# A mixture-of-experts tail: where the one-hot selection, the scatter-adds and the loads of the sums stand in the queues

## The chip, the cores and the metric

One Trainium2 chip, one of its cores. The metric is the device time of one execution in microseconds (us), of which the median of several runs is given. Engines are called TensorE (PE in the profile), VectorE (DVE), ScalarE (ACT), GpSimd (POOL) and SyncE (SP). TensorE has a second row, PEld, for its weight loads. Each engine takes its instructions in order from a queue of its own; SyncE's and POOL's queues also issue the DMA transfers.

## The reference

One block of a streaming encoder over 512 tokens of width 1024 in float32: a mixer of two branches (chunked retention and sparse attention), then a hierarchical mixture of experts, then a last RMSNorm. The change concerns the experts and the last norm:

```python
# u2: normalized tokens; 16 experts in 4 groups; top group, then its top 2 experts
gates = einsum('tke,tk->te', one_hot(eid, 16), wts)      # zero for 14 of 16 experts
a = einsum('td,edf->tef', xb, w1)                         # 1024 -> 256
b = einsum('td,edf->tef', xb, w3)
hid = silu(a) * b * gb[:, :, None]
y   = einsum('tef,efd->td', hid, w2)                      # 256 -> 1024
h = h + g2 * y
out = rmsnorm(h, norm_final_g)
```

Each token goes to two experts, so an expert has 64 tokens on the average. The weights of one expert are 3 MB (w1, w3 and w2 of 1 MB each).

## The kernel before

**Planner.** The kernel records its instructions in a list and does not emit them as they are written. A planner (`Program.run`) gives each one an engine time and a DMA time from a table of costs (`cost`), plays the whole list through in its own model of the engines and the DMA, and so fixes for every engine the order of its queue and for every tile the place in on-chip memory. Lower `prio` (recorded earlier) goes first among instructions that could start at about the same time. A tile has a "tag" with places for it; places of different phases may overlap, and a later phase opens when the tiles of the earlier one are done. What the planner assumes of time decides only the order; on the chip each queue waits for what is really ready.

**Router.** For each of four blocks of 128 tokens the kernel computes the block's sum `hh` (stored to `hrow` in DRAM, 512 rows of 1024) and the normalized tokens (stored to `u2row` as a high and a low half in float16), and picks experts. At its end, `row_all` holds for each expert the list of its token numbers (128 slots, unused ones out of bounds) and `gate_all` the gates.

**Experts.** The loop at L1334 runs over 16 experts. `load` fetches an expert's weights from SyncE's queue as three tiles of 1 MB (two with half of w1 and w3 each, one with w2) and splits each on ScalarE and VectorE into two float16 parts. `compute` gathers the expert's tokens from `u2row` by an indirect DMA from POOL's queue into one of six buffers `xg`, transposes them, runs gate and up matmuls, SiLU and product, two transposes, the down matmuls, and scales the result into a tile `y`. `add` is an indirect DMA from POOL that adds the rows of `y` to the rows of `hrow` that `row` names (a scatter-add). `hrow` is split into four views so that experts which follow each other use different views; two scatter-adds to one view wait for each other.

In the kernel before, only the scatter-adds of experts 0 and 1 (in loop order) are issued as they come. Those of 2 to 14 are kept in a list `late` and recorded behind an instruction `gated` on POOL that reads the last expert's w2 tile, so that they start when the last weights have arrived:

```python
1338        if i == E - 1 and late:
1339            R.hold = gated = POOL.tensor_copy(gate[0:1, 0:1], raw[0:1, 0:1])
1340            for a in late:
1341                add(*a)
...
1344        if 2 <= i < E - 1:
1345            late.append((y, row, hrow_of[e // 4]))
```

The tiles `y` that wait for them have nine places (three, two, and four over the buffers `xg`).

**The last expert** has no scatter-add. Its `y` stays on chip and is added by a matmul with a one-hot selection: `last` holds the numbers 0 to 511 along the row (`iota` on POOL, a copy to float on VectorE), and `at_last` is 1 where that number equals the token number in a slot of the last expert (`is_equal` on VectorE). These instructions are recorded after the loop (L1353 to L1359).

**Branch.** At L1367 every engine reads the number of rounds; L1368 branches over a block that serves experts with more than 128 tokens. With this input the block is skipped. Instructions behind it are planned on their own.

**Final norm** (L1388 to L1407), for each block of 128 tokens: SyncE loads the sums from `hrow`, TensorE multiplies the selection by `y` (float32), VectorE adds the product to the sums, ScalarE squares and sums, POOL takes the power -0.5, and VectorE, ScalarE and POOL scale the block, which SyncE stores.

Of the kernel before, what the change touches and what calls it, by code (L numbers as in the profile page):

```python
# [11 lines left out]
F32 = mybir.dt.float32  # L12
F16 = mybir.dt.float16
I32 = mybir.dt.int32
AF = mybir.ActivationFunctionType
OP = mybir.AluOpType
# [4 lines left out]
S = 512  # L21
D = 1024
KT = D // 128
NT = S // 128
H = 8
E = 16
# [122 lines left out]
class Program:  # L149
# [149 lines left out]
    def cost(self, op, method, a, k, reads, writes):  # L299
        ap = lambda v: v.ap if isinstance(v, View) else v  # L300
        ps = lambda v: isinstance(v, View) and v.buf.tag.space == "PS"
        op.dma = 0.0
        out = ap(writes[0])
        n = shape_of(out)
        if "dma" in method:
            tot = cnt = 0
            for v in (writes[0], [r for r in reads][0]):
                x = ap(v)
                e = mybir.dt.size(x.dtype)
                tot_v = 1  # L310
                for c in x.shape:
                    tot_v *= c
                tot = tot_v if not tot else min(tot, tot_v)
                run = x.shape[-1] if list(x.ap)[-1][0] == 1 else 1
                cnt = max(cnt, tot_v / run)
            tot *= mybir.dt.size(out.dtype)
            op.dma = max(tot, cnt * 157) / 360.0
            op.dur = 1040.0 if "indirect" in method else 550.0
            return
        if op.eng == "PE":  # L320
            op.share = 1.0
            f32 = ap(reads[0]).dtype == F32
            if method == "transpose":
                op.dur = 109.0 if f32 else 56.0
            else:
                op.dur = max(27.0, n / 2.4 * (4 if f32 else 1) + 2.5)
                if f32 and (n < 128 or out.shape[0] == 64):
                    op.dur = 117.0
                op.share = min(1.0, n / 2.4 * (4 if f32 else 1) / op.dur)
            return  # L330
        big = max([n] + [shape_of(ap(r)) for r in reads if r is not None])
        scal = sum(1 for r in reads[1:] if shape_of(ap(r)) == 1 and n > 1)
        if op.eng == "ACT":
            op.dur = (52.0 if ps(reads[0]) else 93.0) + big / 1.2 + 93 * scal + (93 if "accum_out" in k else 0)
            func = a[2] if len(a) > 2 else k["func"]
            op.table = TABLE.get(func)
        elif op.eng == "DVE":
            two = sum(1 for r in reads if shape_of(ap(r)) > 1) > 1
            half = all(ap(r).dtype == F16 for r in reads)
            fast = not two and (half or not any(ps(v) for v in reads)) and method in ("tensor_scalar", "tensor_copy", "memset")  # L340
            op.dur = 69.0 + big * (0.52 if fast else 1.042) + 61 * min(1, scal)
        else:
            if k.get("op") == OP.pow:
                op.dur = 300 + 165.0 * n
            elif method in ("memset", "iota", "tensor_scalar"):
                op.dur = 60 + 0.87 * n
            else:
                op.dur = 150 + 2.1 * n
# [150 lines left out]
KB = 1024  # L499
ARENA = 207 * KB  # L500
NXG = 6


def block(ctx, tc, A, out):
# [3 lines left out]
    dram = ctx.enter_context(tc.tile_pool(name="scratch", bufs=1, space=DRAM))  # L508
# [3 lines left out]
    R = Program(tc, arena, banks)  # L512
    R.TABLE_COST = 300
    T = R.tile
# [3 lines left out]
    def stt(o, a, s, b, op0, op1, **k):  # L518
        return DVE.scalar_tensor_tensor(o, a, s, b, op0=op0, op1=op1, **k)
# [12 lines left out]
    hrow = dram.tile([S, D], F32, name="hrow")  # L532

    hrow_of = dram_disjoint_views(hrow, 4)

    x_t = A["x"].rearrange("b (t p) d -> (b t) p d", p=128)
    w_in = A["w_in"].rearrange("l (k p) n -> p (l k) n", p=128)
# [10 lines left out]
    def fixed(shape, dt=F32, phase=0, n=1):  # L548
        size = (2 if dt == F16 else 4) * int(np.prod(shape))
        size += -size % 32  # L550
        t = R.tag("SB", size, (place[phase], n, phase))
        place[phase] += n * size
        return T(t, shape, dt) if n == 1 else t
# [40 lines left out]
    tHH = R.tag("SB", 4 * KB, (U, 2, 4))  # L594
    tG1 = R.tag("SB", 4 * KB, (TMP + 32 * KB, 1, 3))
    tVEC = R.tag("SB", 4 * KB, (U + 16 * KB, 3, 4))
    tT4 = R.tag("SB", 4 * KB, (U + 28 * KB, 3, 4), (U + 40 * KB, 2, 5), (U, 4, 6))
    tWX = R.tag("SB", 8 * KB, (TMP + 64 * KB, 1, 3), (U + 40 * KB, 1, 3), (U + 8 * KB, 1, 4))
    tT4H = R.tag("SB", 4 * KB, (TMP + 40 * KB, 4, 4))
    tSA = R.tag("SB", 2 * KB, (TMP + 36 * KB, 2, 4))  # L600
# [690 lines left out]
    def load(es, early=0):  # L1291
        R.shift, R.low = early, True
        c13 = [split(echunk(w1[:, es, q * 4:q * 4 + 4], w3[:, es, q * 4:q * 4 + 4]), view=paired) for q in range(2)]
        raw = echunk(w2[:, es])
        c2 = split(raw)
        R.shift, R.low = 0, False
        return c13, c2, raw
# [30 lines left out]
    def add(y, row, rows):  # L1328
        POOL.indirect_dma_start(out=rows[:, :], out_offset=Off(row), in_=y, in_offset=None,
                                bounds_check=S - 1, oob_is_err=False, compute_op=OP.add)  # L1330


    late, gate = [], fixed([1])
    for i in range(E):  # L1334
        e = i % 4 * 4 + i // 4
        row = row_all[:, e:e + 1]
        *w, raw = load(slice(e, e + 1), 300 if i < 5 else -50)
        if i == E - 1 and late:
            R.hold = gated = POOL.tensor_copy(gate[0:1, 0:1], raw[0:1, 0:1])
            for a in late:  # L1340
                add(*a)
            R.hold = None
        y = compute(*w, row, gate_all[:, e:e + 1], xg[i % NXG], T(tG1, [D]) if i == E - 1 else None)
        if 2 <= i < E - 1:
            late.append((y, row, hrow_of[e // 4]))
        elif i < E - 1:
            add(y, row, hrow_of[e // 4])

    R.hold = gated
    gfb = T(tVEC, [D])  # L1350
    row_load(gfb, A["norm_final_g"][None, :])
    R.hold = None
    last = T(tVEC, [2, S])  # L1353
    POOL.iota(last[:, 0].bitcast(I32), pattern=[[1, S]], base=0, channel_multiplier=0)
    DVE.tensor_copy(last[:, 1], last[:, 0].bitcast(I32))
    rowf = fixed([1])
    DVE.tensor_copy(rowf, row)
    at_last = last[:, 0]
    DVE.tensor_scalar(at_last, last[:, 1], rowf, None, op0=OP.is_equal)  # L1359
    R.keep(gfb)  # L1360
    R.keep(last)
    assert place[0] <= 8 * KB and place[4] <= ARENA, place
    R.run()

# [1 line left out]
    R.immediate = True  # L1366
    nr = nc.values_load(R.real(nri[0:1, 0:1]), min_val=1, max_val=ROUNDS)  # L1367
    with tc.If(nr > 1):  # L1368
        with tc.For_i(1, nr):
            DVE.tensor_scalar(rank, rank, -128.0, None, op0=OP.add)  # L1370
            pr, pg = psf(), psf()
            for t in range(NT):
                locate(pr, t, val, F16, t == 0, t == NT - 1)
                locate(pg, t, gval, F32, t == 0, t == NT - 1)
            take(pr, pg)
            SP.dma_start(more_row.rearrange("n p -> p n"), row_all)
            SP.dma_start(more_gate.rearrange("n p -> p n"), gate_all)
            with tc.For_i(0, E) as e:
                row, gt = row_all[:, 0:1], gate_all[:, 0:1]
                SP.dma_start(row, more_row.rearrange("n p -> p n")[:, bass.ds(e, 1)])  # L1380
                SP.dma_start(gt, more_gate.rearrange("n p -> p n")[:, bass.ds(e, 1)])
                add(compute(*load(bass.ds(e, 1))[:2], row, gt, xg[0]), row, hrow)
    R.immediate = False


    R.patience = 100
    o_t = out.rearrange("b (t p) d -> (b t) p d", p=128)
    for t in range(NT):  # L1388
        h3 = T(tW8, [2, D], F32, "h")
        SP.dma_start(h3[:, 0], hrow[t * 128:(t + 1) * 128, :])  # L1390
        for n in range(2):
            d = slice(n * 512, (n + 1) * 512)
            p = (psm, psm, psa, psf)[t]()
            PE.matmul(p, at_last[:, t * 128:(t + 1) * 128], y[:, d], start=True, stop=True)
            DVE.tensor_add(h3[:, 0, d], h3[:, 0, d], p)
            ACT.activation(h3[:, 1, d], h3[:, 0, d], AF.Square, accum_out=s3[:, t, n:n + 1])
        DVE.tensor_scalar(s3[:, t, 0:1], s3[:, t, 0:1], 1.0 / D, 1e-6, op0=OP.mult, op1=OP.add)
        stt(s3[:, t, 1:2], s3[:, t, 1:2], 1.0 / D, s3[:, t, 0:1], OP.mult, OP.add)
        POOL.tensor_tensor(s3[:, t, 1:2], s3[:, t, 1:2], mhalf, op=OP.pow)
        for n in range(2):  # L1400
            d = slice(n * 512, (n + 1) * 512)
            if n and t < NT - 1:
                ACT.activation(h3[:, 1, d], h3[:, 0, d], AF.Copy, scale=s3[:, t, 1:2])
                POOL.tensor_mul(h3[:, 1, d], h3[:, 1, d], gfb[:, d])
            else:
                stt(h3[:, 1, d], h3[:, 0, d], s3[:, t, 1:2], gfb[:, d], OP.mult, OP.mult)
            SP.dma_start(o_t[t][:, d], h3[:, 1, d])  # L1407
    R.run()


# [20 lines left out]
```

## Time and profile before

| | before |
|---|---|
| median of 3 runs | 722.64 us (719.57, 722.64, 724.06) |
| profiled execution | 719.95 us |
| span of its profile, first to last instruction | 718.1 us |
| busy: TensorE, VectorE, ScalarE, POOL | 638.4, 552.3, 375.7, 100.3 us |
| mean granted TensorE clock | 0.956 |
| DMA moved | 151.93 MB, 212 GB/s over the span |

How to read the lines that follow: the page has one line for each group of equal instructions and a table in which the span is cut into 40 equal slices (a digit is the busy share in tenths). A line of the timeline has start, duration, engine, source line, operation, output and input with their shapes, count, and in brackets how long the engine had stood idle before and what released it. All tiles on chip are named arena, all accumulators banks; nearly every instruction carries line L494, where the planner emits it. A line of the table of windows has, for a stretch of time, the busy time and count of each engine, then the granted clock, the mean busy share of the 16 DMA engines and the GB/s.

### The profile page before, as it was taken

How to read it: one execution, taken by the hardware profiler on the slowest of the kernel's cores; microseconds unless marked ns; L12 is line 12 of the kernel's file. 1: busy time of each engine (PE TensorE's matmuls, PEld its weight loads, DVE VectorE, ACT ScalarE, POOL GpSimd, SP SyncE). 2: the span in 40 equal slices, each digit the busy share in tenths (PEclk: the TensorE clock that was granted, in tenths of full speed). 3: DMA queues.
4: the chain of work that ended last, by engine and by line, in shares of the span. 5: the costliest groups of instructions: out<-in, count | busy, mean ns of one | idle time of the engine just before them, and what ended most of it. 6: DMA issues, size and time to landing. Idle time of an engine off the chain costs nothing. (4 is left out here: it accounts for less than half of the span.)

```text
span 718.1 us, 10181 instructions
## 1 busy us (share of the span) xinstructions
PE 638.4 (89%) x3673; PEld 345.5 (48%) x3673; DVE 552.3 (77%) x1056; ACT 375.7 (52%) x605; POOL 100.3 (14%) x87
## 2 busy tenths in 40 slices
PE   3799998989999999999799999989559989999942
PEld 2345465747565644555354444435244445555410
DVE  3997699999994677989588545778764788899726
ACT  5457623333253356773475432544347578899304
POOL 1001010111011100000000000041642201102733
PEclk9799999999999999999999999999859999999987
DMA  9998525272265278657758435824628899997546
GB/s 298 359 341 240 170 68 153 64 221 84 73 208 157 78 252 257 222 177 269 217 197 302 177 118 178 327 82 159 222 84 306 273 354 357 375 346 279 101 87 233
DMA packets 85255, 151.93 MB, mean 212 GB/s; under 512 B 10433, under 2 KB 50834, under 8 KB 85074
## 3 DMA queue, kind: packets, MB, share of 16 engines
q1 hardware_dynamic: 80690, 143.21, 59.6%
q0 software_dynamic: 4464, 8.04, 4.7%
q8 instruction: 29, 0.48, 0.3%
q14 instruction: 24, 0.20, 0.1%
q10 hardware_dynamic: 48, 0.00, 0.0%
HBM read 137.91 MB, written 16.81 MB: 215 GB/s over the span
## 5 line engine op out<-in xcount | busy, mean ns | idle before, releaser
L494 PE MATMUL banks<-arena 128*128 128x512 f16 (+9 forms) x3673 | 638.4, 335 | 66.4 <-DVE arena L494 43.3
L494 PEld LDWEIGHTS <-arena 128*128 128x128 f16 x3078 | 282.1, 100 | 289.1 <-issue 32.9
L494 ACT ACTIVATE arena<-arena 128x1024 f16<-128x1024 f32 (+8 forms) x320 | 258.1, 846 | 192.1 <-DVE arena L494 94.0
L494 DVE SCALAR_TENSOR_TENSOR arena<-arena 128x1024 f16<-128x1024 f32 (+7 forms) x318 | 294.0, 949 | 62.9 <-ACT arena L494 48.4
L494 ACT ACTIVATE arena<-banks 128x512 f32<-128x512 f32 (+7 forms) x178 | 99.3, 604 | 106.7 <-PE banks L494 105.5
L494 DVE SCALAR_TENSOR_TENSOR arena<-banks,arena 128x512 f32<-128x512 f32 (+9 forms) x147 | 89.2, 629 | 44.6 <-PE banks L494 30.7
L494 PEld LDWEIGHTS banks<-arena 128*128 128x128 f32 (+2 forms) x595 | 69.3, 168 | 69.4 <-DVE arena L494 38.0
L494 POOL TENSOR_TENSOR arena<-arena 128x512 f32<-128x512 f32 (+2 forms) x36 | 41.7, 1160 | 291.5 <-DVE arena L494 237.3
L494 DVE TENSOR_TENSOR arena<-arena 128x512 f32<-128x512 f32 (+6 forms) x100 | 56.0, 571 | 9.2 <-POOL arena L494 5.8
L494 ACT ACTIVATE arena<-banks,arena 128x128 f32<-128x128 f32 (+1 forms) x48 | 22.9, 531 | 37.1 <-DVE arena L494 25.1
L494 DVE TENSOR_SCALAR arena<-arena 128x1 f32<-128x1 f32 (+7 forms) x76 | 22.6, 328 | 11.8 <-ACT arena L494 5.7
L494 POOL DMA_INDIRECT hrow<-arena x15 | 26.3, 1753 | 19.6 <-DVE arena L494 15.3
L494 DVE MAX8 arena<-arena 128x8 f32<-128x256 f32 (+3 forms) x52 | 27.6, 530 | 1.4
L494 POOL DMA_INDIRECT arena<-u2row,arena x16 | 19.3, 1208 | 62.6 <-PE banks L494 50.1
L494 POOL IOTA arena<- 128x4 int32 (+2 forms) x3 | 1.5, 502 | 188.8 <-PE banks L494 188.7
L494 DVE MATCH_REPLACE8 arena<-arena 128x256 f32<-128x256 f32 (+3 forms) x56 | 27.2, 487 | 0.0
L494 DVE SCALAR_TENSOR_TENSOR arena<-arena,banks 128x512 f32<-128x512 f32 x17 | 11.6, 685 | 7.0 <-PE banks L494 4.5
L494 DVE CUSTOM_DVE_ANT_0 arena<-arena 128x128 f32<-128x128 f32 (+3 forms) x32 | 14.3, 483 | 0.0
L494 POOL MEMSET arena<- 128x2048 f16 (+2 forms) x12 | 11.0, 955 | 7.3 <-PE banks L494 5.0
L494 ACT ACTIVATION_READ_ACCUMULATOR arena<-arena 128x1 f32 x56 | 10.5, 188 | 0.0
L494 DVE TENSOR_TENSOR arena<-arena,banks 128x512 f32<-128x512 f32 (+1 forms) x12 | 6.0, 512 | 5.6 <-DMA arena<-hrow 5.5
L494 DVE BATCH_NORM_STATS2 arena<-banks 128x6 f32<-128x128 f32 x32 | 7.1, 285 | 3.3 <-PE banks L494 3.2
(19 smaller groups left out, 37.4 us busy)
## 6 DMA issues: line engine op xcount, KB each, us to landing
arena<-in_w_ada SPq DMA_DIRECT2D x16, 1024.0 KB
arena<-in_w_exp_gate SPq DMA_DIRECT2D x32, 512.0 KB
arena<-in_w_exp_up SPq DMA_DIRECT2D x32, 512.0 KB
arena<-in_w_exp_down SPq DMA_DIRECT2D x16, 1024.0 KB
arena<-in_w_in SPq DMA_DIRECT2D x14, 1024.0 KB
arena<-in_w_ada SPq DMA_DIRECT2D x4, 2048.0 KB
arena<-in_w_gate SPq DMA_DIRECT2D x8, 1024.0 KB
arena<-arena SPq DMA_DIRECT2D x112, 64.0 KB
```

Of the source, the lines that this page charges most:

```text
L494: o.call(*[self.real(x) for x in o.args], **{n: self.real(x) for n, x in o.kw.items()})
```

## The change

It does six things.

1. The one-hot selection of the last expert (`iota`, copy, `is_equal`) is recorded ahead of the loop over the experts, from the last column of `row_all`.
2. `late` stays empty: each of the 15 scatter-adds is recorded right behind its expert.
3. The loads of the sums from `hrow` become four tiles `ha`, recorded behind the loop and ahead of the branch, in a place of 16 KB that the gather buffers `xg` 2 to 5 leave free; so experts 14 and 15 gather into `xg` 0 and 1, and the tiles `y` lose the four places there.
4. The final norm works on `ha` and keeps only its output in a tile of its own.
5. In the skipped block, later rounds add into a second DRAM table `mrow`, which is then added to `ha`.
6. The planner counts half the DMA time for an indirect transfer.

```diff
@@ cost
-            op.dma = max(tot, cnt * 157) / 360.0
+            op.dma = max(tot, cnt * 157) / 360.0 * (0.5 if "indirect" in method else 1.0)
@@ tags
-    tT4 = R.tag("SB", 4 * KB, (U + 28 * KB, 3, 4), (U + 40 * KB, 2, 5), (U, 4, 6))
+    tT4 = R.tag("SB", 4 * KB, (U + 28 * KB, 3, 4), (U + 40 * KB, 2, 5))
+    tHA = R.tag("SB", 4 * KB, (U, 4, 6))
@@ ahead of the loop
+    last = T(tVEC, [2, S])
+    POOL.iota(last[:, 0].bitcast(I32), pattern=[[1, S]], base=0, channel_multiplier=0)
+    DVE.tensor_copy(last[:, 1], last[:, 0].bitcast(I32))
+    rowf = fixed([1])
+    DVE.tensor_copy(rowf, row_all[:, E - 1:E])
+    at_last = last[:, 0]
+    DVE.tensor_scalar(at_last, last[:, 1], rowf, None, op0=OP.is_equal)
@@ loop over the experts
-        if i == E - 1 and late:
+        if i == E - 1:
             R.hold = gated = POOL.tensor_copy(gate[0:1, 0:1], raw[0:1, 0:1])
...
-        y = compute(*w, row, gate_all[:, e:e + 1], xg[i % NXG], T(tG1, [D]) if i == E - 1 else None)
-        if 2 <= i < E - 1:
+        y = compute(*w, row, gate_all[:, e:e + 1], xg[i % NXG if i < 14 else i - 14], T(tG1, [D]) if i == E - 1 else None)
+        if 15 <= i < E - 1:
             late.append((y, row, hrow_of[e // 4]))
...
-    last = T(tVEC, [2, S])
-    POOL.iota(last[:, 0].bitcast(I32), pattern=[[1, S]], base=0, channel_multiplier=0)
...
-    DVE.tensor_scalar(at_last, last[:, 1], rowf, None, op0=OP.is_equal)
+    ha = [T(tHA, [D]) for _ in range(NT)]
+    for t in range(NT):
+        SP.dma_start(ha[t], hrow[t * 128:(t + 1) * 128, :])
@@ final norm
-        h3 = T(tW8, [2, D], F32, "h")
-        SP.dma_start(h3[:, 0], hrow[t * 128:(t + 1) * 128, :])
+        h3, o3 = ha[t], T(tW8, [D], F32, "h")
...
-            DVE.tensor_add(h3[:, 0, d], h3[:, 0, d], p)
+            DVE.tensor_add(h3[:, d], h3[:, d], p)
```

More of the change, by code (lines that the diff above doesn't have):

```diff
@@ L534, in block @@
     hrow_of = dram_disjoint_views(hrow, 4)
+    mrow = dram.tile([S, D], F32, name="mrow")
     x_t = A["x"].rearrange("b (t p) d -> (b t) p d", p=128)
@@ L1352, in block @@
     R.hold = None
-    last = T(tVEC, [2, S])
-    POOL.iota(last[:, 0].bitcast(I32), pattern=[[1, S]], base=0, channel_multiplier=0)
[L1355 to L1358, printed above, removed]
-    DVE.tensor_scalar(at_last, last[:, 1], rowf, None, op0=OP.is_equal)
-    R.keep(gfb)
-    R.keep(last)
+    ha = [T(tHA, [D]) for _ in range(NT)]
+    for t in range(NT):
+        SP.dma_start(ha[t], hrow[t * 128:(t + 1) * 128, :])
+    for v in (gfb, last, *ha):
+        R.keep(v)
     assert place[0] <= 8 * KB and place[4] <= ARENA, place
@@ L1368, in block @@
     with tc.If(nr > 1):
+        zero = T(tW8, [D])
+        DVE.memset(zero, 0.0)
+        for t in range(NT):
+            SP.dma_start(mrow[t * 128:(t + 1) * 128, :], zero)
         with tc.For_i(1, nr):
@@ L1381, in block @@
                 SP.dma_start(gt, more_gate.rearrange("n p -> p n")[:, bass.ds(e, 1)])
-                add(compute(*load(bass.ds(e, 1))[:2], row, gt, xg[0]), row, hrow)
+                add(compute(*load(bass.ds(e, 1))[:2], row, gt, xg[0]), row, mrow)
+        for t in range(NT):
+            m = T(tW8, [D])
+            SP.dma_start(m, mrow[t * 128:(t + 1) * 128, :])
+            DVE.tensor_add(ha[t], ha[t], m)
     R.immediate = False
@@ L1394, in block @@
             PE.matmul(p, at_last[:, t * 128:(t + 1) * 128], y[:, d], start=True, stop=True)
-            DVE.tensor_add(h3[:, 0, d], h3[:, 0, d], p)
-            ACT.activation(h3[:, 1, d], h3[:, 0, d], AF.Square, accum_out=s3[:, t, n:n + 1])
+            DVE.tensor_add(h3[:, d], h3[:, d], p)
+            ACT.activation(o3[:, d], h3[:, d], AF.Square, accum_out=s3[:, t, n:n + 1])
         DVE.tensor_scalar(s3[:, t, 0:1], s3[:, t, 0:1], 1.0 / D, 1e-6, op0=OP.mult, op1=OP.add)
@@ L1402, in block @@
             if n and t < NT - 1:
-                ACT.activation(h3[:, 1, d], h3[:, 0, d], AF.Copy, scale=s3[:, t, 1:2])
-                POOL.tensor_mul(h3[:, 1, d], h3[:, 1, d], gfb[:, d])
-            else:
-                stt(h3[:, 1, d], h3[:, 0, d], s3[:, t, 1:2], gfb[:, d], OP.mult, OP.mult)
-            SP.dma_start(o_t[t][:, d], h3[:, 1, d])
+                ACT.activation(o3[:, d], h3[:, d], AF.Copy, scale=s3[:, t, 1:2])
+                POOL.tensor_mul(o3[:, d], o3[:, d], gfb[:, d])
+            else:
+                stt(o3[:, d], h3[:, d], s3[:, t, 1:2], gfb[:, d], OP.mult, OP.mult)
+            SP.dma_start(o_t[t][:, d], o3[:, d])
     R.run()
```

## The prediction, made before the changed kernel ran

> **What bounds the kernel now.** I read the page's head and its table of 40 slices first. A slice is 18 us; the digits are busy tenths.
>
> ```profile
> span 718.1 us, 10181 instructions
> ...
> PE   3799998989999999999799999989559989999942
> ...
> DMA  9998525272265278657758435824628899997546
> ...
> GB/s 298 359 341 240 170 68 153 64 221 84 73 208 157 78 252 257 222 177 269 217 197 302 177 118 178 327 82 159 222 84 306 273 354 357 375 346 279 101 87 233
> ```
>
> From slice 32 to slice 35 (574 to 646 us, in the expert stage) TensorE is at 8 or 9 and the DMA engines are at 9. Then the DMA row falls to 7, 5, 4, and TensorE's to 4 and 2 in the last two slices: there is an end in which nobody works much. A table of windows says how much:
>
> ```profile
> 541.00:660.00 119.00, 114.73 (x679) 59.18 (x678) 95.85 (x110) 94.56 (x116) 15.08 (x12) 0.99 0.93 341
> 660.00:684.00 24.00, 23.50 (x131) 11.38 (x129) 17.43 (x22) 11.58 (x16) 18.42 (x11) 1.00 0.49 87
> 684.00:691.00 7.00, 0.00 (x0) 0.00 (x0) 1.58 (x4) 0.05 (x1) 3.91 (x4) 0.83 0.58 103
> ```
>
> Until 660 the DMA engines are 93% busy with expert weights (341 GB/s). From 660 to 684 TensorE works off a backlog (23.50 of 24 us) while the DMA moves 87 GB/s. From 684 to 691 TensorE does nothing at all. The timeline of that end names who holds what:
>
> ```profile
> 659.74 0.98 POOL L494 COPY arena<-arena 1x1 f32<-1x1 f32 x1 [43.79 <-ACT arena L494]
> ...
> 660.90 2.43 POOL L494 DMA_INDIRECT hrow<-arena  x1 [0.17 <-DVE arena L494]
> ...
> 673.05 1.22 DVE L494 SCALAR_TENSOR_TENSOR arena<-arena 128x1024 f16<-128x1024 f32 x1
> ...
> 678.92 0.75 DVE L494 SCALAR_TENSOR_TENSOR arena<-banks,arena 128x512 f32<-128x512 f32 x1 [1.26 <-PE banks L494]
> ...
> 683.67 0.38 ACT L494 ACTIVATE arena<-banks 128x256 f32<-128x256 f32 x1 [6.46 <-PE banks L494]
> 687.24 1.55 POOL L494 DMA_INDIRECT hrow<-arena  x1 [0.93 <-DMA hrow<-arena]
> 688.24 1.15 POOL L494 IOTA arena<- 128x512 int32 x1
> 689.42 0.43 DVE L494 CAST arena<-arena 128x512 f32<-128x512 int32 x1 [9.75 <-POOL arena L494]
> 689.76 0.74 DVE L494 SCALAR_TENSOR_TENSOR arena<-banks,arena 128x512 f32<-128x512 f32 x1
> ...
> 690.79 1.57 POOL L494 DMA_INDIRECT hrow<-arena  x1 [1.40 <-DVE arena L494]
> 690.82 0.41 DVE L494 SCALAR_TENSOR_TENSOR arena<-banks,arena 128x256 f32<-128x256 f32 x1
> ...
> 696.71 0.75 DVE L494 SCALAR_TENSOR_TENSOR arena<-banks,arena 128x512 f32<-128x512 f32 x1 [0.33 <-PE banks L494]
> 697.65 7.13 PE L494 MATMUL banks<-arena 128*128 128x512 f32 x16 [0.98 <-DVEq L1368]
> 699.15 1.77 SPq L494 DMA_DIRECT2D arena<-hrow  x4
> ...
> 703.01 1.28 DVE L494 TENSOR_TENSOR arena<-arena,banks 128x512 f32<-128x512 f32 x2 [5.54 <-DMA arena<-hrow]
> ...
> 711.62 3.08 DVE L494 SCALAR_TENSOR_TENSOR arena<-arena 128x512 f32<-128x512 f32 x3 [0.33 <-POOL arena L494]
> ```
>
> Thirteen scatter-adds start at 660.90, once the last expert's down weights have arrived (the COPY at 659.74 waits for them), and leave one after the other; the twelfth is issued at 687.24. Behind it in POOL's queue stands the iota for the one-hot selection. VectorE reached the copy of that iota after 679.67 and stood 9.75 us. Behind the copy in VectorE's queue waited (a) the second half of expert 14's output, issued at 689.76, without which the last scatter-add could not leave at 690.79, and (b) the last expert's SiLU product, ready when ScalarE was done at 684.05 and run only at 690.82. Then two things join in the first addition at 703.01: the sums by token, loaded at 699.15 after the last scatter-add had landed, and the selection matmuls from 697.65. The load is the later one (VectorE idle 5.54 us, released by DMA arena<-hrow). From 703.01 to the end of the span is 15.1 us of final norm and stores. So the end is bound by a queue: scatter-adds, iota, copy, expert 14, scatter-add, load.
>
> **The change part by part.**
>
> *The selection moves to the router's end.* Three operations leave the end: iota (1.15 us), its copy (0.43) and the comparison (0.47). At the router's end POOL and VectorE have these gaps:
>
> ```profile
> 529.51 1.83 POOL L494 DMA_INDIRECT arena<-u2row,arena  x1 [10.31 <-DVE arena L494]
> 539.91 2.36 DVE L494 SCALAR_TENSOR_TENSOR arena<-arena 128x1024 f16<-128x1024 f32 x2 [5.06 <-ACT arena L494]
> ```
>
> POOL was idle 10.31 us ahead of the first gather, VectorE 5.06 us ahead of 539.91. Lower bound of the cost 0, upper 2.05 us if all three stood one behind the other on the router's chain; I take 0, because those gaps are longer. If they were placed inside the router's dependent chain instead, the 2.05 us would be paid once. What goes: (a) expert 14's second half runs about 1.3 us after its first, at 680.3, not 689.76; (b) the last SiLU product runs at 684.1, not 690.82, and everything that follows from it (transposes, down projection, 697.46) comes 6.7 us earlier: output complete at 690.75, selection matmuls from 690.95, the first sum possible at 691.9 (two of the sixteen, 7.13 us for all).
>
> *Every scatter-add is issued at once.* The number of scatter-adds stays 15; thirteen lose the wait for the last weights and run behind their expert's output, on POOL between the gathers. The last one then leaves at about 680.5, and lands as before:
>
> ```profile
> L494 POOL DMA_INDIRECT hrow<-arena x15: 1552/1569/2426, 554.4 to 690.8; - x15
> ...
> DMA to landing us min/median/max: 5.9/9.2/9.8
> ```
>
> It took 8.3 us from 690.79 to the loads' issue at 699.15 (the rows above: 5.9 to 9.8, median 9.2). So the loads could go at about 688.9, less if fewer scatter-adds are in flight.
>
> *The loads of the sums stand ahead of the branch.* The same four; the first one's data came 3.86 us after issue (699.15 to 703.01), so at 692.7. SyncE then passes the branch behind them; behind it a consumer waits on the producer's own event at the branch, as the selection matmuls do above (released by DVEq L1368):
>
> ```profile
> L1368 SPq EVENT_SEMAPHORE  x8: 17/17/17, 657.1 to 661.2; - x8
> L1368 DVEq EVENT_SEMAPHORE  x1: 21/21/21, 697.6 to 697.6; - x1
> ```
>
> SyncE's eight collect the loads in flight, from 657.1 to 661.2; VectorE's is one of 21 ns. Bounds for the first addition: 0 if it waits only for its own load, 3.0 us more if for all four (the rest of 2 MB at the roughly 400 GB/s below takes about that). I take 0.8, nearer to the first, as the eight are passed one by one in order.
>
> *What the scatter-adds do to the weight stream.* This is the cost. They used to run when DMA was half idle; now eleven of them (experts 2 to 12) fall into the stream ahead of the last gate and up load. What one costs in engine time:
>
> ```profile
> 556.00:560.00 4.00, 4.00 (x20) 1.86 (x19) 3.48 (x5) 2.46 (x4) 1.11 (x2) 1.00 0.38 74
> 560.00:564.00 4.00, 4.00 (x40) 2.68 (x38) 3.64 (x5) 2.84 (x5) 2.15 (x2) 1.00 0.91 271
> 564.00:568.00 4.00, 4.00 (x21) 1.79 (x19) 3.34 (x5) 3.52 (x4) 0.94 (x1) 1.00 0.95 228
> 568.00:572.00 4.00, 4.00 (x24) 2.00 (x23) 3.12 (x3) 1.06 (x1) 0.00 (x0) 1.00 1.01 403
> 584.00:588.00 4.00, 4.00 (x21) 1.92 (x20) 3.95 (x5) 2.16 (x3) 0.00 (x0) 1.00 0.97 329
> ```
>
> The first scatter-add ran nearly alone from 556 to 560: 0.38 of 4 us, so 1.5 us. The second was in flight beside weights from 560 to 568: 7.44 us of busy time (0.91 and 0.95 of 4 us) for 2.0 MB, where the rate of the next row (403 at 1.01, so 399 GB/s) needs 5.0. Lost 2.4 us, plus 0.66 for its own quarter of a MB: 3.1 at most. The row 584 to 588 loses 0.6 without a scatter-add, in a burst of new loads, so 2.5 is fairer; a gather was in flight as well. I take 2.2, nearest to that loaded row. Eleven of them: 24 us of engine time; of the 8.3 us that the engines idled between 541 and 660 I let 3 be filled. The last gate and up load came about 657.1 (1 MB of down weights, 2.6 us at 399 GB/s, ahead of 659.74) and comes about 678. Behind it lie two halves to split (1.05 us on ScalarE, 1.22 on VectorE each, some 3.5 in a pipe) and six matmuls: TensorE could end the last expert's gate and up at 683.5, and its own backlog ends at 683.64. **The cover is the 24 us backlog of TensorE, and it is just used up.** The down weights land one load later and are needed only at 685.7. On top, one stall of this kind has been seen:
>
> ```profile
> 573.53 2.00 ACT L494 ACTIVATE arena<-arena 128x1024 f16<-128x1024 f32 x2 [3.29 <-DMA arena<-in_w_exp_gate]
> 576.32 24.03 PE L494 MATMUL banks<-arena 128*128 128x128 f32 x132 [3.18 <-DVE arena L494]
> ```
>
> ScalarE stood 3.29 us at the head of its queue for a weight load, a SiLU waited behind it, and TensorE lost 3.18 us. With later loads this comes back; bounds 0 and several times 3.2. I take 2 us in all.
>
> The Trainium skill, page "DMA: Bandwidth & Descriptors", section "Issuing engines are not separate DMA queues", says that DMAs from whatever engine end on the same 16 engines and interleave. It speaks against the change, and the trace agrees (228 GB/s at a 0.95 share beside a scatter-add, 403 without). Were it otherwise, the stream would not move and the sum below would be that of the first rival.
>
> *The planner's figure* (half the transfer time for indirect DMAs), the places of buffers and the second table for later rounds add no instruction to this run; they reorder queues. Bounds plus and minus 2 us; I take 0.
>
> *Sum.* TensorE's path: 691.9 + 2 = 693.9. The loads' path: 692.7 + 2 = 694.7. The later decides, and 0.8 for the branch: 695.5 against 703.01, **7.5 us earlier**; the 15.1 us behind it are unchanged (the last selection matmul would end near 700, before the last addition needs it). The profiled execution took 719.95 (span 718.1): 712.5. The median of the three runs is 722.64, 2.7 above the profiled one, so I forecast **715.1**. A measurement of this kernel tells about 1% (7.2 us) from no change, so the forecast lies on that line.
>
> **The rivals.**
>
> *The scatter-adds are nearly free.* At 1.5 us each the last gate and up load comes at 671, the backlog covers it, no stall: first addition at 692.7 to 693.6, 9.4 to 10.3 earlier, 712.3 to 713.2; with the 573 stall gone too, 709. For: the lone scatter-add. Against: the loaded row. Chance 0.14.
>
> *Half eaten.* At 2.5 to 3.1 us each the last load comes at 682 to 688, gate and up end 4 to 10 us late, first addition at 696 to 702: 1 to 6 earlier, 717 to 722. Chance 0.15.
>
> *The loads do not come early.* If expert 14's down projection is put behind the last gate and up matmuls, or its scatter-add behind another wait on POOL, it leaves near 687 and lands near 695; the first addition comes at 699.5, 3.5 earlier, 719. Then the sums are not "loaded during the last expert" at all. For: already in the best case they arrive 2 us after its output. Chance 0.12.
>
> *Slower: the weight stream becomes the bound.* Place: ScalarE's splits, ahead of SiLUs in one queue. Price: 3.1 us for each scatter-add (first addition at 701.7) and two stalls of 3.2: 708.1, 5.1 later, 728. It decides from about 3.2 us a scatter-add without stalls. For: DMA at 0.93 for 119 us. Against: 24 us of backlog at 660, and TensorE busy for 114.73 of the 119 us before it. Chance 0.19.
>
> **How the numbers follow.** The forecast (6 to 9 us earlier, 713.6 to 716.6) has 0.40. Faster by over 1%: 0.14, and 0.29 of the forecast's: 0.43. Slower by over 1% needs 730: 0.13 of the last rival. Within 1%: the rest, 0.44. The range goes from 709.5 (all free, no stall) to 725 (half of the slow case): about 8 in 10.
>
> **What would show it.** The copy of the iota stands near 530, and VectorE's 9.75 us are gone. Scatter-adds lie between 554 and 685, none queued behind another. The DMA share from 560 to 675 stays above 0.95 at a lower weight rate, and the last weights land 15 to 25 us later than 659.74. TensorE still ends its long run at 684 to 687. The first addition is at 693 to 697, released by a load or by the branch. I am wrong if TensorE shows waits for ScalarE or VectorE from 600 to 684 that add to over 4 us, or if the last scatter-add leaves after 685.

## The result: 1.2% slower, and the profile after

The median after is 729.32 us (nine runs, 725.44 to 732.5) beside 722.03 for the kernel before in the same comparison (nine runs, 716.83 to 724.06). The ratio is 1.0122, 95% interval 1.0084 to 1.016. The forecast was 715.1 with a range up to 725.0: the time lies 4.3 us beyond the range, on the slower side. The profiled execution took 726.23 us, with a span of 724.2 (before 719.95 and 718.1).

The page after: the same rows of the table of slices (18.1 us each) as shown of before, and the group of the scatter-adds.

```profile
span 724.2 us, 10192 instructions
...
PE   4699998989999998999799999988569897899893
...
DMA  8998524272365379658577446734547998999525
...
L494 POOL DMA_INDIRECT hrow<-arena x15 | 33.1, 2208 | 105.5 <-DVE arena L494 105.5
```

Before, TensorE was at 9 from slice 33 to 37 and thin in the last two (4 and 2). Now slices 33, 34 and 37 (from 597, 615 and 670 us) are at 7, 8 and 8, and the work goes on into slice 38 (9). The DMA row is down to 5 and then 2 in slices 37 and 38, where before it had fallen to 7 and 5 in 36 and 37. Each of the scatter-adds waited for VectorE, that is for its own expert's output (105.5 us of POOL's time over 15), and none for another scatter-add.

The end of TensorE's work and the first addition, from the timeline after:

```profile
674.86 26.70 PE L494 MATMUL banks<-arena 128*128 128x512 f16 x126 [0.24 <-ACT arena L494]
...
680.85 2.95 ACT L494 ACTIVATE arena<-arena 128x1024 f16<-128x1024 f32 x3 [1.41 <-DMA arena<-in_w_exp_down]
...
697.87 1.55 POOL L494 DMA_INDIRECT hrow<-arena  x1 [4.98 <-DVE arena L494]
701.59 0.38 ACT L494 ACTIVATE arena<-banks 128x256 f32<-128x256 f32 x1 [6.72 <-PE banks L494]
702.01 0.42 DVE L494 SCALAR_TENSOR_TENSOR arena<-banks,arena 128x256 f32<-128x256 f32 x1 [4.41 <-ACT arena L494]
...
704.10 2.57 SPq L494 DMA_DIRECT2D arena<-hrow  x4
...
707.60 1.40 DVE L494 TENSOR_TENSOR arena<-arena,banks 128x512 f32<-128x512 f32 x2 [0.65 <-DMA arena<-hrow]
...
710.18 0.69 DVE L494 TENSOR_TENSOR arena<-arena,banks 128x512 f32<-128x512 f32 x1 [0.90 <-SPq L1374]
```

The queue at the end is gone, as forecast: the last expert's SiLU (701.59) is followed by its product after 0.42 us, the last scatter-add leaves at 697.87, and the first addition stands 6.04 us behind the end of TensorE's long run (674.86 + 26.70 = 701.56, to 707.60). Before, that distance was 19.4 us (683.63 to 703.01). So the end became 13.3 us shorter. But the long run ends 17.9 us later, and the stretch behind the first addition grew from 15.1 to 16.6 us. 17.9 - 13.3 + 1.5 = 6.1 us, which is the difference of the spans.

The windows of the same work, from the router's end to the end of the long run, before and then after, show where the 17.9 us are:

```profile
541.00:683.70 142.70, 138.23 (x808) 70.56 (x806) 113.28 (x131) 105.84 (x131) 33.37 (x22) 0.99 0.86 299
```
```profile
541.00:701.60 160.60, 143.02 (x812) 71.45 (x809) 115.59 (x132) 107.65 (x133) 44.93 (x25) 0.96 0.81 270
```

TensorE's share of these windows is the third number. Before it stood still for 142.70 - 138.23 = 4.5 us, after for 17.6: 13.1 us more. The other 4.8 us are busy time at a lower granted clock (0.96 beside 0.99; 138.23 x 0.99 and 143.02 x 0.96 are the same work, 137). The timeline of TensorE after shows the places:

```profile
576.36 27.61 PE L494 MATMUL banks<-arena 128*128 128x128 f32 x167 [2.31 <-DVE arena L494]
608.45 20.39 PE L494 MATMUL banks<-arena 128*128 128x512 f16 x106 [4.48 <-ACT arena L494]
632.25 18.40 PE L494 MATMUL banks<-arena 128*128 128x128 f32 x108 [3.42 <-ACT arena L494]
652.46 0.98 PE L494 MATMUL banks<-arena 128*128 128x128 f32 x6 [1.81 <-ACT arena L494]
...
673.64 0.98 PE L494 MATMUL banks<-arena 128*128 128x128 f32 x6 [2.75 <-ACT arena L494]
```

The bracket is the idle time ahead of each stretch: 2.31, 4.48, 3.42, 1.81 and 2.75 us, together 14.8; behind 576.32 the kernel before had none until 683.63. All but the first were released by ScalarE. What ScalarE was doing says its own timeline:

```profile
604.26 2.95 ACT L494 ACTIVATE arena<-arena 128x1024 f16<-128x1024 f32 x3 [4.59 <-DMA arena<-in_w_exp_down]
607.11 2.19 ACT L494 ACTIVATE arena<-banks 128x256 f32<-128x256 f32 x3
...
627.11 3.90 ACT L494 ACTIVATE arena<-arena 128x1024 f16<-128x1024 f32 x4 [4.68 <-DMA arena<-in_w_exp_down]
...
648.27 2.95 ACT L494 ACTIVATE arena<-arena 128x1024 f16<-128x1024 f32 x3 [4.03 <-DMA arena<-in_w_exp_down]
...
669.45 2.95 ACT L494 ACTIVATE arena<-arena 128x1024 f16<-128x1024 f32 x3 [3.92 <-DMA arena<-in_w_exp_down]
```

Four times the same picture. ScalarE stands 3.9 to 4.7 us at the head of its queue for down weights (128x1024 f16: a split), and right behind stand the SiLUs (as at 607.11: they read the accumulators, banks, 128x256) for which TensorE waits. The waits from 529 to 700, first of after, then of before:

```profile
ACT arena L494 <- DMA arena<-in_w_exp_down: 22.5, 8, 4.7
```
```profile
ACT arena L494 <- DMA arena<-in_w_exp_down: 1.2, 1, 1.2
```

### The profile page after: what moved, and what is told of

Same layout as the page of the kernel before. It is cut to its first block, busy times and chain, and to the rows that moved or that the text cites. A ratio compares the mean times of both kernels' runs of the same rounds, so it can differ in the third digit from the quotient of the medians.

```text
span 724.2 us, 10192 instructions
## 1 busy us (share of the span) xinstructions
PE 640.5 (88%) x3673; PEld 345.4 (48%) x3673; DVE 554.4 (77%) x1056; ACT 375.6 (52%) x605; POOL 107.4 (15%) x87
## 2 busy tenths in 40 slices
DMA packets 85255, 151.93 MB, mean 210 GB/s; under 512 B 10433, under 2 KB 50834, under 8 KB 85074
## 5 line engine op out<-in xcount | busy, mean ns | idle before, releaser
L494 DVE SCALAR_TENSOR_TENSOR arena<-banks,arena 128x256 f32<-128x256 f32 (+9 forms) x147 | 90.0, 630 | 53.7 <-PE banks L494 32.5
L494 POOL DMA_INDIRECT hrow<-arena x15 | 33.1, 2208 | 105.5 <-DVE arena L494 105.5
L494 ACT ACTIVATE arena<-banks,arena 128x128 f32<-128x128 f32 (+1 forms) x48 | 23.0, 531 | 36.0 <-DVE arena L494 23.9
L494 DVE SCALAR_TENSOR_TENSOR arena<-arena,banks 128x512 f32<-128x512 f32 x17 | 11.6, 686 | 7.3 <-PE banks L494 4.8
L494 DVE TENSOR_TENSOR arena<-banks,arena 128x256 f16<-128x256 f32 x16 | 6.8, 423 | 8.9 <-ACT arena L494 8.8
```

Source lines behind the costliest of these rows:

```text
L494: o.call(*[self.real(x) for x in o.args], **{n: self.real(x) for n, x in o.kw.items()})
```

## The experiments

The letters A to D are those of the expectations, which say what each theory holds. Ratios are to the kernel before, run on the same chip beside each, with a 95% interval. The runs are spread over several chips, on which the median of the kernel before was 720.0 to 722.2 us, so a difference of two medians below is good to some 2 us.

**Is it the scatter-adds' traffic, or what else was moved?** e1_no_rows:

```diff
-    bounds_check=S - 1, oob_is_err=False, compute_op=OP.add)
+    bounds_check=0, oob_is_err=False, compute_op=OP.add)
```

> The changed kernel, with the scatter-adds' row limit set to 0: every engine's queue is the same, each scatter-add is issued and completes, but moves at most one row instead of about 64 (the sums by token stay without the experts). Theory A (traffic): the rows of the scatter-adds beside the weight stream make the loads of the down weights late, ScalarE waits for them with a SiLU behind, TensorE starves. Then ScalarE's 22.5 us of waits for down weights fall below 6 us, TensorE's long run ends at 684 to 689 instead of 701.6, and the time is 709 to 716. Theory B (order): the new queue order itself makes the splits block ScalarE, traffic or not. Then the waits stay at 15 to 22 us, TensorE ends at 697 or later, and the time is 722 to 729.

Measured: 702.53 us, ratio 0.9737 (0.9695 to 0.9779). TensorE's timeline and ScalarE's waits of that run:

```profile
653.32 25.01 PE L494 MATMUL banks<-arena 128*128 128x512 f16 x126 [0.24 <-ACT arena L494]
```
```profile
ACT arena L494 <- DMA arena<-in_w_exp_down: 8.3, 6, 2.5
```

With every instruction in the same place in its queue and the rows not moved, TensorE's long run ends at 678.33, 23.2 us earlier than after, and the time falls by 26.8 us. That is a larger gain than its theory A gave (709 to 716), and the waits are 8.3 us where A had below 6. So the traffic is the cause of the loss. e1 lies 18.4 us below the kernel before (720.92 beside it, less 702.53), but that is not what the change would be worth without the loss: the kernel before moves the rows too, at its end, and e1 moves none.

**Is it the order that the planner chose?** e2_full_cost takes the halved figure back; e5_slack3 and e6_slack6 let the planner believe that the experts' weights land 3 or 6 us later than it thought, so that it places a split less tightly. No instruction is added.

```diff
 e2: -  op.dma = max(tot, cnt * 157) / 360.0 * (0.5 if "indirect" in method else 1.0)
     +  op.dma = max(tot, cnt * 157) / 360.0
 e5: -  o.fin = dq + self.DMA_DONE
     +  o.fin = dq + self.DMA_DONE + (3000.0 if o.low else 0.0)     # e6: 6000.0
```

> The changed kernel with the planner's old figure for indirect DMAs (1.46 us instead of 0.73 us): only the order of the queues changes. Theory A (traffic): the traffic is the same, so the waits for down weights stay at 15 us or more; the time is 722 to 732. Theory B (order): with the old figure the planner expects later loads and puts the splits behind the SiLUs; waits below 8 us, 712 to 719.

> The changed kernel, with one figure of the planner changed: it takes the experts' weight loads to land 3 us later than before. On the chip nothing is slower; only the splits of fresh weights stand further back in ScalarE's and VectorE's queues. Theory A (a load made late by the scatter-adds blocks a SiLU that stands behind its split): the waits for down weights fall from 22.5 us to below 8, TensorE's long run ends at 685 to 692 instead of 701.6, 710 to 719. Rival C (the scatter-adds take throughput of the DMA engines that the weights need, whatever the order): waits move elsewhere, TensorE ends near 700, 724 to 731.

> As the run before with 6 us in place of 3. Theory A: no stall is left, but weight buffers are held longer in the plan; 708 to 720. Rival C: 724 to 733.

Measured: e2 725.28 us, ratio 1.0045 (1.0012 to 1.0078); e5 720.51, 1.0001 (0.9956 to 1.0045); e6 723.05, 1.0024 (0.9984 to 1.0063). In e5 ScalarE still waits for down weights:

```profile
ACT arena L494 <- DMA arena<-in_w_exp_down: 23.3, 7, 4.9
```

Theory A's number for e5 (below 8 us) was missed. The times of e5 and e6 lie between the ranges: above A's (710 to 719 and 708 to 720), below C's (724 and more). In e2 the time is in A's range, but the waits fell to 11.4 us, where A had 15 or more and B below 8. The order is worth 4 to 9 us of the 27; no order tried gets the rest back.

**One part at a time.** e3_selection_only is the kernel before with only the selection moved ahead of the loop. e4_selection_late8 is e3 with the scatter-adds of six more experts at once. e7_at_once_only is the kernel before with only the scatter-adds at once.

```diff
 e3: the lines of `last`, `rowf` and `at_last` ahead of the loop, from row_all[:, E - 1:E]
 e4: e3, and -  if 2 <= i < E - 1:   +  if 8 <= i < E - 1:
 e7: before, and -  if i == E - 1 and late:   +  if i == E - 1:
                 -  if 2 <= i < E - 1:        +  if 15 <= i < E - 1:
```

> The kernel before with the one-hot selection alone moved to the router's end; scatter-adds are still held until the last weights are there. VectorE's wait of 9.75 us goes and the last SiLU product runs at about 684.1, but the thirteen scatter-adds leave 2.5 us apart as before, so the last one leaves at about 689.7 instead of 690.8 and the first addition comes at about 702: 1 us gained, 719 to 723. If instead VectorE's wait was what bound the end, 712 to 716.

> As the run with the selection alone, but only the scatter-adds from the ninth expert on are held: six more run beside the weight stream, seven remain for the end. Theory A: each one beside the stream costs about a third of what thirteen cost (17.9 us of TensorE's end), so some 3 to 8 us of stalls against about 8 us gained at the end: 714 to 724. Theory B (order): no stalls, the chain of the held ones ends near 681, first addition at about 694: 709 to 714.

> The kernel before with the scatter-adds issued at once and nothing else: the selection stays behind the loop, the sums are loaded behind the branch, the planner keeps its old figure. Theories A and C alike: the traffic is that of the changed kernel, and so are the stalls; TensorE ends at 695 to 702, and the end gains less than in the changed kernel since the loads come behind the branch: 722 to 732. If a part other than the scatter-adds made the changed kernel slow, 708 to 716.

Measured: e3 719.22 us, ratio 0.9979 (0.9947 to 1.0012); e4 721.41, 0.9976 (0.9941 to 1.0012); e7 722.95, 1.0027 (0.9993 to 1.006). The end of e3:

```profile
656.82 2.62 POOL L494 DMA_INDIRECT hrow<-arena  x1 [0.17 <-DVE arena L494]
...
685.40 1.55 POOL L494 DMA_INDIRECT hrow<-arena  x1 [0.94 <-DVE arena L494]
...
694.87 1.77 SPq L494 DMA_DIRECT2D arena<-hrow  x4
698.49 1.29 DVE L494 TENSOR_TENSOR arena<-arena,banks 128x512 f32<-128x512 f32 x2 [12.40 <-DMA arena<-hrow]
```

With the iota gone, the thirteen held scatter-adds themselves are the queue, from 656.82 to 685.40, about 2.4 us apart, and the sums arrive 12.40 us after VectorE was ready for them. So the wait that the prediction put first was not worth its 9.75 us by itself. (The profiled execution of e3 took 715.29 us, 3.9 below its median, so this profile shows more gain than the runs do.) The end of e7:

```profile
680.94 17.54 PE L494 MATMUL banks<-arena 128*128 128x512 f16 x76 [2.87 <-ACT arena L494]
...
708.09 1.28 DVE L494 TENSOR_TENSOR arena<-arena,banks 128x512 f32<-128x512 f32 x2 [4.21 <-DMA arena<-hrow]
```

TensorE's work ends at 698.48 (before 683.63) and the first addition stands at 708.09: the loss in the stream is there without any of the other edits. e4, with half of the scatter-adds early, ends TensorE's work at 696.4 already, against 680.7 in e3. The three medians lie in the ranges expected (of theory A for e4). e7 and e2, which is the whole change with the same planner's figure, differ by no more than their intervals (1.0027 and 1.0045): beside the scatter-adds at once, the selection and the early loads gain nothing that these runs can tell.

**What in a scatter-add costs?** e8_plain_write writes the rows and adds nothing; e12_half_rows moves half of them.

```diff
 e8:  -  bounds_check=S - 1, oob_is_err=False, compute_op=OP.add)
      +  bounds_check=S - 1, oob_is_err=False)
 e12: -  bounds_check=S - 1,   +  bounds_check=S // 2 - 1,
```

> The changed kernel with scatter-adds turned into plain scatters: the same rows are written, but the rows of the sums are not read and not added. All queues are the same. If the price beside the weight stream is that of the bytes written, the stalls stay and the time is 722 to 729. If it is that of reading the sums and adding, most of it goes: 706 to 714.

> The changed kernel, scatter-adds limited to the tokens 0 to 255: about half of the rows move (the sums of the other tokens stay without the experts), all queues the same. If the price is a sum of engine time (theory C), it goes with the rows: half of the 27 us between 729 and 702.5 is gained, 713 to 718. If it is a matter of a few late loads beyond a threshold (theory A), it is not half: 703 to 709 or 723 to 728.

Measured: e8 713.84 us, ratio 0.9889 (0.9812 to 0.9966); e12 718.13, 0.9955 (0.9923 to 0.9986). Of the 26.8 us between after and e1, plain writes give 15.5 back (four runs, good to some 5 us), half of the rows 11.2. So about half of the price or more is that the sums are read and added, and it goes roughly with the number of rows. e8 lies in the range for reading and adding, although ScalarE still waits 15.6 us for down weights; e12 lies just beyond theory C's 713 to 718 and outside both of A's ranges. From issue to landing, in after and in e8 (least, median, most; e1, which moves hardly a row, has a median of 8.0):

```profile
DMA to landing us min/median/max: 6.0/10.5/11.5
```
```profile
DMA to landing us min/median/max: 3.8/8.1/9.7
```

**Does it add up with the weights?** e13_half_down leaves all scatter-adds as after and loads half of each expert's down weights.

```diff
+    SP.dma_start(raw[:, 0:1024] ...)   <- w2[:, es, 0:1]; the split reads that half twice
-    raw = echunk(w2[:, es])
```

> The changed kernel with all its scatter-adds, but of each expert's down weights only the first half is loaded (0.5 MB less for each expert, about 1.3 us of engine time; the second half of the tile is split from the first half's data, so the result uses wrong down weights there). All queues and the planner's figures are the same. Theory C (the scatter-add's 1.5 us of engine time and the weights add up on the same engines): taking 1.3 us away from the weights is worth nearly as much as taking the scatter-adds' rows away: waits for down weights below 10 us, 703 to 711. If it is something of the scatter-adds themselves (their reads and writes slowing a load's last packets), the stalls stay: 718 to 727.

Measured: 713.37 us, ratio 0.9862 (0.9819 to 0.9905), 16.0 us below after. The run moved 8.4 MB less (143.54 beside 151.93), which takes 21 us at the 399 GB/s of the prediction. The waits for down weights fell to 7.3 us, as C expected, but its 703 to 711 us were not reached; nor does the time lie in the rival's range. Some three quarters of the DMA time taken out of the weights come back. (The profiled executions of e12 and e13, 711.99 and 717.39 us, lie some us from their medians; only medians are used of them, beside the waits.)

**Is it the number of tiles that wait for TensorE?** e9_tile_less takes one of the 14 places of 8 KB away, e10_tile_more adds one in place of gather buffers.

```diff
 e9:  -  ..., (TMP, 4, 3), (TMP + 56 * KB, 1, 4), (Y, 2, 5))   +  ..., (TMP, 4, 3), (Y, 2, 5))
 e10: +  ..., (U + 8 * KB, 1, 5))     NXG = 4, and tXG with (U, 2, 5)
```

> The changed kernel with 13 instead of 14 weight tiles of 8 KB in the expert stage (the one in the former w_o area is left out). Theory D (closed loop: a load is issued only when TensorE has freed a tile, so TensorE's work behind the last load is the tiles' worth and no slack, and every us a load takes longer is paid by TensorE): TensorE's end behind the last down load falls by about half an expert (4 us), but the loop turns slower: 6 to 14 us slower than the changed kernel, 735 to 743. Rival C (the DMA engines' throughput alone binds): they were busy 0.90 to 0.92 of the stage; with one tile less they stay so, 726 to 732.

> The changed kernel with 15 weight tiles in the expert stage, the place taken from two of the six gather buffers. Theory D: each load is issued about half an expert earlier and late landings are covered better; TensorE ends 4 to 10 us earlier, 718 to 725. Rival C: no change, 726 to 732.

Measured: e9 728.8 us, ratio 1.0124 (1.0062 to 1.0187), the same as after; e10 725.24, 1.006 (1.0024 to 1.0095). D's number for e9 (735 to 743) missed, C's hit; e10 lies between the ranges of the two. One tile more or less is no cure.

**When may they run?** e11_release1, e11_release2 and e14_release3 are e3 with the held scatter-adds released by the down weights of the expert one, two or three places before the last (12, 11 and 10 held).

```diff
-        if i == E - 1 and late:
+        if i == E - 1 - h and late:          # h = 1, 2, 3
-        if 2 <= i < E - 1:
+        if 2 <= i < E - 1 - h:
```

> The kernel before with the selection at the router's end, and the held scatter-adds released by the down weights of the last expert but one instead of the last (twelve are held, expert 14's is issued as it comes). They start 8 to 10 us earlier, beside the last three loads only, behind which no load waits for a tile. Theory D: those three loads come up to 6 us later, the backlog of TensorE covers it, and the chain of scatter-adds ends 6 to 9 us earlier than the 694.9 of the selection alone: first addition at 690 to 694, 711 to 716. Rival C: what the chain gains is paid by the loads, 717 to 722.

> The same released one expert earlier still (eleven held). Theory D: now six loads run beside the scatter-adds, and the first three of them still hold others back: 712 to 720. Rival C: 718 to 724.

> The kernel before with the selection at the router's end and the held scatter-adds released by the down weights of the expert three before the last (ten held). Nine loads are then issued beside scatter-adds. Where the release at one and at two experts before the last gave 711.8 and 712.3, the price of holding back loads that others wait for must show from some point on: 714 to 722. If the scatter-adds' engine time is covered as long as they come late in the stage, 710 to 714.

Measured: h = 1 711.77 us, ratio 0.9887 (0.9818 to 0.9956); h = 2 712.34, 0.988 (0.9828 to 0.9931); h = 3 726.83, 1.0096 (1.0062 to 1.013). The timeline of h = 1, then of h = 3:

```profile
578.47 82.78 PE L494 MATMUL banks<-arena 128*128 128x512 f16 x519 [2.14 <-ACT arena L494]
...
649.51 0.24 POOL L494 COPY arena<-arena 1x1 f32<-1x1 f32 x1 [27.77 <-DMA arena<-in_w_exp_down]
...
681.55 1.55 POOL L494 DMA_INDIRECT hrow<-arena  x1 [0.94 <-DMA hrow<-arena]
...
691.03 1.78 SPq L494 DMA_DIRECT2D arena<-hrow  x4
694.50 1.29 DVE L494 TENSOR_TENSOR arena<-arena,banks 128x512 f32<-128x512 f32 x2 [6.38 <-DMA arena<-hrow]
```
```profile
629.88 2.42 POOL L494 DMA_INDIRECT hrow<-arena  x1 [0.17 <-DVE arena L494]
...
648.75 0.38 SPq L494 DMA_DIRECT2D arena<-in_w_exp_down  x1
...
663.64 2.95 ACT L494 ACTIVATE arena<-arena 128x1024 f16<-128x1024 f32 x3 [7.86 <-DMA arena<-in_w_exp_down]
...
675.11 1.06 ACT L494 ACTIVATE arena<-arena 128x1024 f16<-128x1024 f32 x1 [6.62 <-SPq L1369]
...
676.95 10.14 PE L494 MATMUL banks<-arena 128*128 128x128 f32 x47 [12.72 <-DVE arena L494]
...
681.38 2.95 ACT L494 ACTIVATE arena<-arena 128x1024 f16<-128x1024 f32 x3 [2.36 <-SPq L1369]
```

With h = 1 the last scatter-add leaves at 681.55 instead of 685.40 and the first addition is at 694.50 instead of 698.49; TensorE shows no hole from 578 to 661 and one of 0.58 us until its long run ends at 682.72: it has work behind the last loads. h = 1 and h = 2 came out in theory D's ranges. h = 3 did not: 726.83 lies above the 714 to 722 expected, and not for the reason expected. No load was held back there: the last down load is issued at 648.75, in e3 at 648.14. But the loads landed late. ScalarE stands 7.86 us for down weights, then 6.62 and 2.36 us at later splits (put down to SyncE's events at the branch, which the prediction read as collecting the loads in flight), and TensorE stands 12.72 us. The last split starts 32.6 us after the last load's issue; before, 7.4 us lie between that issue and the COPY that reads the weights (652.38 to 659.74). The DMA engines were meanwhile busy 72% of the time from 650 to 660 and 47 to 58% from 660 to 676. Why loads land so late on engines that are half idle is not shown. The versions with h = 1 and 2 are 1.1 to 1.2% faster than the kernel before and 2.3 to 2.4% below the changed one (711.77 and 712.34 beside 729.32).

## Why the prediction was wrong

**Right: the end, and more than that.** The iota has moved to the router's end (forecast: near 530):

```profile
515.76 0.55 POOL L494 IOTA arena<- 128x512 int32 x1
```

VectorE's wait of 9.75 us is gone and no scatter-add is queued behind another. The end shortened by 13.3 us where the sum had 7.5, of which it had taken off 2 for a stall and 0.8 for the branch. Some 2 us of the rest is the last scatter-add: 6.2 us from it to the loads (697.87 to 704.10), where the 8.3 of before had been taken. The branch's 0.8 came near by luck and at another place: the first addition stood 0.65 us for its load, and then the next one 0.90 us for SyncE's events (L1374), within a tail that is 1.5 us longer. (Its upper bound of 3.0 us was too small: three more loads of 0.5 MB take 3.9 at the 399 GB/s that the prediction used.)

**Wrong: the cover.** The step that failed is "The cover is the 24 us backlog of TensorE, and it is just used up." The lateness that it was to cover came as forecast: the last down weights come at 680.85 instead of 659.74, 21 us later, where 15 to 25 had been given. But TensorE's long run did not end at 684 to 687; it ended at 701.56. A backlog of that kind is there behind the last load in all three runs: 23.9 us before (659.74 to 683.63), 20.7 after (680.85 to 701.56), at least 18.7 in e1 (weights there by 659.6, end at 678.33). It moved with the load and was not spent on it. When the last down load was issued, after and then before, shows why:

```profile
669.30 0.38 SPq L494 DMA_DIRECT2D arena<-in_w_exp_down  x1
```
```profile
652.38 0.38 SPq L494 DMA_DIRECT2D arena<-in_w_exp_down  x1
```

A load is issued when its tile has been freed, and from 560 to 680 SyncE waited mostly for TensorE's reads to free one (72.6 us after, 51.3 before, 66.0 in e1). TensorE stood in the middle of the stream, behind ScalarE's waits, so the loads behind were issued later: of the 21 us the last down load has 16.9 already at its issue, and 4.2 more in flight (11.6 instead of 7.4). What TensorE lost there no backlog at the end can give back. That the backlog is the depth of the weight tiles is how I read it; e9, with one tile less and the same time, does not bear it out. How far the cover reaches is open as well: releases at h = 1 and 2 were covered, h = 3 was not, and there the loads were late in landing and not in issue.

The prediction had named what would prove it wrong, and both came: waits of TensorE from 600 to 684 over 4 us (12.5: 4.48, 3.42, 1.81, 2.75) and a last scatter-add after 685 (697.87).

**Mis-sized: the stall.** "I take 2 us in all" stood for what is 13.1 us more of standing and 4.8 us of lower clock. The mechanism was named (a split that waits for a load at the head of ScalarE's queue, a SiLU behind it), in the bounds as "several times 3.2" and as the slower rival, with 728 us and a chance of 0.19. It is this rival that came: 729.32 us, and a first addition at 707.60 where it had 708.1. That its number was so near is luck: it had 3.1 us for each scatter-add and two stalls, and the runs have 1.5 us and four. Its condition was off too: it was to decide from about 3.2 us a scatter-add, and it decided at half of that.

**Mis-sized the other way: the price of one.** Forecast 2.2 us of DMA engine time. The windows of after and of e1, whose queues are the same:

```profile
541.00:660.00 119.00, 104.69 (x608) 53.09 (x606) 87.38 (x100) 85.44 (x104) 35.03 (x19) 0.96 0.90 305
660.00:672.00 12.00, 10.89 (x73) 5.86 (x71) 10.05 (x12) 7.39 (x10) 3.70 (x3) 1.00 0.95 351
672.00:681.00 9.00, 7.12 (x27) 3.07 (x28) 6.27 (x8) 7.59 (x11) 0.33 (x1) 0.81 0.71 244
```
```profile
541.00:660.00 119.00, 116.39 (x693) 59.47 (x691) 103.28 (x118) 100.31 (x123) 42.78 (x23) 1.00 0.90 328
660.00:672.00 12.00, 11.77 (x68) 5.79 (x67) 8.59 (x11) 5.15 (x8) 2.52 (x3) 1.00 0.01 1
```

The share is the number before the last. After: 0.90 x 119 + 0.95 x 12 + 0.71 x 9 = 124.9 us busy; e1 until its weights are in: 0.90 x 119 + 0.01 x 12 = 107.2. The difference of 17.7 us over the twelve scatter-adds up to 668 is 1.5 us each, the figure of the lone one and of the rival "nearly free". That rival was to bring 709 to 713 us at 1.5: the price was right there and the cover wrong. So the 21 us of lateness were met by luck. The prediction had made them of 24 us of engine time less 3 of idle time filled; against the 0.93 x 119 = 110.7 of before, the engines were busy 14 us longer and idle 7 us longer until the last weights were in.

**Wrong: the sign to look for.** The DMA share was to stay above 0.95 from 560 to 675. It was 0.93 there, and 0.90 from 541 to 660, lower than before (0.93). e1, whose TensorE hardly stands, has 0.90 from 541 to 660 as well: the share alone does not tell a stalled stream from a free one.

**The planner's figure** was taken at 0, plus or minus 2: e2 puts it at 4.0 us (729.32 against 725.28), or 5.5 by the ratios.

The Trainium skill, page "DMA: Bandwidth & Descriptors", section "Rules for kernel authors", says that an accumulating DMA reads its destination and writes it later. No run here shows the read as such; what they show is its price: 729.32 us with, 713.84 us without the accumulation.

**Open.** How lateness passes from load to load was read from the traces and not isolated: from 600 to 640 the DMA engines were 13% idle (a share of 0.87) while TensorE stood, in e9 one tile less, which should have hurt if the depth alone decided, did not, and in h = 3 the loads landed late beside half idle engines. Each edit that moves the planner shifts orders by a few us, which these runs can't separate from the edit itself.

## What to carry to other kernels

Work queued behind the last load of a ring of buffers is not slack of the whole stream: here it was 23.9 us before and 20.7 after, while the stream's end moved by 18 us. Before transfers are moved beside a stream, ask what stands behind the instruction that waits for the stream's loads in its queue, and sum engine time over the whole stretch (here 13 x 1.5 us against DMA engines at 0.93 and TensorE at 0.96). Releasing held transfers one or two steps before the stream's end made the kernel 1.1 to 1.2% faster than before; three steps made it 1.0% slower.

## What the hardware showed unexpectedly

A stall can cost TensorE more than its idle time. Windows of after, behind the holes at 608.45 and 632.25 (after the ten numbers of the engines come the granted clock, the share and the GB/s):

```profile
608.45:612.00 3.55, 3.55 (x12) 1.79 (x13) 2.17 (x3) 3.34 (x5) 0.00 (x0) 0.50 0.90 282
612.00:616.00 4.00, 4.00 (x16) 1.65 (x15) 2.32 (x3) 2.56 (x3) 0.00 (x0) 0.79 0.58 235
...
632.25:636.00 3.75, 3.75 (x22) 2.04 (x23) 2.92 (x5) 3.75 (x5) 0.00 (x0) 1.00 1.03 338
```

Behind 4.48 us of standing the granted clock was 0.50 for 3.55 us and 0.79 for 4: 1.8 + 0.8 = 2.6 us lost on top. Behind 3.42 us at 632.25 it was 1.00. The Trainium skill, page "TensorE: Matmul & The Clock Gate", section "Part 1: The HAM clock gate", says that the clock halves after an idle window of about 3.4 us and that the windows run freely; both rows agree with that. The prediction left this part of a stall's price out.

A scatter-add of some 64 rows (0.26 MB) took 1.5 us of the 16 engines' time where the weights' rate of 399 GB/s gives 0.66. POOL's own instruction for it grew from 1753 to 2208 ns on the average; the weight loads alone are not the reason, as the one at 690.59, behind the last of them, still took 2.30 us.
